# The passage from the scan to the second feed-forward layer: sums of squares carried on by VectorE, transposes pinned to products, three units by token halves

## The chip, the cores and the metric

One Trainium2 chip, one of its cores. The kernel is one program on one core; its time is the device time of one execution in microseconds (us). The time before is the median of three executions, 740.4 us (739.77 to 740.83). The profile comes from one more execution.

Engines in the rows: PE is TensorE (PEld its weight loads, which overlap), DVE is VectorE, ACT is ScalarE, POOL is GpSimd, SP is SyncE, which here issues the weight DMAs. A row's tile names are the program's; L61 is line 61 of the kernel.

## The reference

A decoder trunk on 256 tokens of width 1024, in float32, two layers. Each layer is a token mixer and then a gated feed-forward with a causal depthwise convolution of width 3. Layer 0 mixes by sparse attention, layer 1 by a state-space scan (SSD). Each of the four sub-layers is wrapped in two RMS norms:

```
m = mixer(rms_norm(h, gains[0]));   h = h + rms_norm(m, gains[1])
f = conv_ffn(rms_norm(h, gains[2])); h = h + rms_norm(f, gains[3])

rms_norm(x, g) = x * rsqrt(mean(x*x, axis=-1) + 1e-6) * g
conv_ffn(h) = (silu(gate) * val) @ w_down,  [val, gate] = causal_dwconv(h @ w_up)
```

The change lies between the scan's output product (`ssd_mixer`'s `y @ w_out`) and the up-products `h @ w_up` of layer 1's feed-forward, whose hidden width is 2816 (22 units of 128 value and 128 gate columns).

## The kernel before, in words

**Arithmetic.** Every float32 operand is split into two float32r parts: `hi` is a rounded copy, made by ScalarE, and `lo = x - hi`, made by VectorE or GpSimd (`split`, line 55). A product of two such operands is three matmuls, hi*hi, hi*lo and lo*hi (`mm3`, line 166). Weights arrive by SP's DMAs in 512 KB parts (128x1024 float32) in five `raw` buffers; each part is split into `whi` and `wlo`. A `raw` buffer is free for the next DMA when its `wlo` has been made. A unit's weights are two parts.

**Tokens.** The 256 tokens are two halves of 128 (half 0 and half 1). `h[0]`, `h[1]` hold the residual stream with tokens on the partitions. The feed-forward needs it with channels on the partitions, so the normed half is transposed by PE (8 transposes of 128x128 in two groups of four, line 152), and the transposed groups are split into `xhi`, `xlo`.

**The passage.** `ssd_out_phase` (line 784) makes the scan's output product in four groups, g = 0 to 3, for half 0 and then half 1; the last stretch does g = 2 and g = 3 together. VectorE adds each group's product, scaled, to `osb` (line 832). For each half, `after` (line 870) then does:

- `postnorm` (line 156): the sum of squares of `osb` in two ScalarE activations of 128x512 (line 126), two GpSimd operations on 128x1 that add the two sums and EPS and take the power -0.5 (lines 117, 119), `fg = osb * gain` in two VectorE operations (line 161), and `h += fg * rstd` in two (line 164);
- `prenorm_steps` (line 141): the same sum of squares on `h`, the same two GpSimd operations, `xn = h * rstd * gain` in two VectorE operations (line 146), and then the transposes and splits.

Half 0's `after` is called before half 1's output products are written down in the program; half 1's `after` behind them.

**The first up-products.** In the feed-forward (`ffn`, line 536) the first two units are done by token halves (`proj_halves`, line 183): both units' products on half 0 (2 x 8 x 3 matmuls of 256 columns, tile `pv`), then half 1's transposes, then both units' products on half 1. A result by halves has tokens on the partitions, so ScalarE copies it to `ut` (line 181) and PE transposes it back (four 128x128 transposes a unit, line 202). All other units are done by `pair` (line 205) on both halves at once, with nothing to transpose.

**What sets the order.** A planner decides at build time in which order each engine gets its instructions: of those whose inputs are ready in its own estimate, it issues the one that stands first in the program's text. Each engine then runs its list strictly in order. `tc.issue_after(ins)` adds only a lower bound: what is written in its block comes behind `ins` in the list of that engine. `pend` (line 861) hands half 1's transposes such bounds: the first two products of the last eight on half 0 (`FB`). Half 0's transposes have no bound in this passage; in the passage from the first feed-forward layer to the scan they are bounded by two of half 1's last five products (`FA`, lines 573 and 574). A layer's tiles lie in a pool that is opened when the pool of the layer before has been closed; both use the same memory.

## Time and profile before

| what | value |
|---|---|
| median of three executions | 740.4 us (739.77 to 740.83) |
| the profiled execution | 737.78 us |
| its span, first to last instruction | 736.0 us |
| granted TensorE clock, mean of the span | 0.993 |
| PE busy | 713.1 us, 97% of the span |
| DVE / ACT / POOL busy | 567.2 / 466.7 / 75.8 us |
| the second feed-forward layer's first product starts | at 541.57 us |
| its last product starts | at 729.32 us |

Read it by stretches: the shares of the whole span are averages over layers with different limits. The `windows` view gives, for each stretch, how long each engine was busy, with the number of instructions in parentheses. The `timeline` view gives single instructions in order of time; a bracket at the end of a row is the time that the engine sat idle before it and what ended that. A row with `x2` merges two that follow each other.

### The profile page before, as it was taken

The page shows a single profiled execution, that of the slowest core. Times are in us where ns is not written, and L with a number is a line of the kernel's source. Part 1 is how long each engine was busy: PE and PEld are TensorE (multiplying, and loading weights), DVE is VectorE, ACT ScalarE, POOL GpSimd, SP SyncE. Part 2 cuts the span into 40 slices and gives each one's busy share as a digit, 9 for nine tenths or more (in the row PEclk, how much of TensorE's full clock was granted, in tenths as well). Part 3 has the DMA queues.
Part 4 walks back from the last instruction along what each step waited for, and adds up shares of the span by engine and source line. Part 5 has one row for each costly group of instructions (what it writes and reads, how often), then busy time and mean ns, then how long its engine had stood idle before and what let it go on. Part 6 is the DMA issues. An engine that isn't in the chain of part 4 may idle for free.

```text
span 736.0 us, 13745 instructions
## 1 busy us (share of the span) xinstructions
PE 713.1 (97%) x5252; PEld 658.0 (89%) x5252; DVE 567.2 (77%) x994; ACT 466.7 (63%) x879; POOL 75.8 (10%) x113
## 2 busy tenths in 40 slices
PE   7998999999999999999999999999989999999996
PEld 4998986779999999997999999998779999999995
DVE  4688898667867777688698878898888877767783
ACT  5577997447656555566776687765647655555551
POOL 2321442120000000001000000133120000000000
PEclk8999999999999999999999999999999999999998
DMA  8865431425655665564445574144655656555531
GB/s 313 297 220 181 140 119 59 142 79 185 199 197 173 193 202 182 195 218 154 139 166 172 181 232 133 58 139 148 200 172 172 200 175 200 197 185 189 181 106 57
DMA packets 35426, 126.07 MB, mean 171 GB/s; under 512 B 4065, under 2 KB 4385, under 8 KB 35361
## 3 DMA queue, kind: packets, MB, share of 16 engines
q1 hardware_dynamic: 35360, 125.20, 51.9%
q8 instruction: 41, 0.67, 0.4%
q14 instruction: 25, 0.20, 0.1%
HBM read 124.14 MB, written 1.05 MB: 170 GB/s over the span
## 4 chain that ended last, share of the span: by engine, by line
PE 77%; DVE 8%; ACT 7%; DMA 4%; issue 2%; POOL 1%; SPq 0%; DVEq 0%; POOLq 0%; ACTq 0%
PE pu L61 45%; PE acc L61 18%; PE pv L61 5%; DVE wlo L57 4%; ACT P L391 2%; PE pt L65 2%; ACT whi L56 2%; PE po L61 2%; ACT junk L126 1%; DMA raw<-in_nsa_in 1%; PE py L61 1%; DMA raw<-in_ffn_down 1%; DMA raw<-in_cmp_w 1%; DVE gw L799 1%; DMA raw<-in_ssd_out 1%
## 5 line engine op out<-in xcount | busy, mean ns | idle before, releaser
L57 DVE TENSOR_TENSOR wlo<-raw,whi 128x1024 fp32r<-128x1024 f32 (+1 forms) x219 | 270.5, 1240 | 79.9 <-ACT whi L56 79.2
L56 ACT CAST whi<-raw 128x1024 fp32r<-128x1024 f32 x223 | 230.8, 1045 | 111.0 <-PE pu L61 56.6
L61 PE MATMUL pu<-xhi,whi 128*128 128x256 f32 x1056 | 296.0, 281 | 1.5 <-DVE graw L288 1.5
L61 PE MATMUL pu<-xhi,wlo 128*128 128x256 f32 x1056 | 295.0, 280 | 1.5 <-DVE wlo L57 1.5
L61 PE MATMUL pu<-xlo,whi 128*128 128x256 f32 x1056 | 294.6, 279 | 0.0
L61 PEld LDWEIGHTS pu<-xhi,whi 128*128 128x128 f32 x1056 | 198.5, 188 | 3.4 <-ACT kd L358 1.6
L61 PEld LDWEIGHTS pu<-xhi,wlo 128*128 128x128 f32 x1056 | 198.4, 188 | 2.2 <-DVE wlo L57 2.1
L61 PEld LDWEIGHTS pu<-xlo,whi 128*128 128x128 f32 x1056 | 198.5, 188 | 1.2
L534 DVE SCALAR_TENSOR_TENSOR cc<-pu,pr,cc 128x255 f32<-128x255 f32 (+2 forms) x248 | 111.3, 477 | 6.7 <-ACT cc L528 3.6
L61 PE MATMUL acc<-whi,hm 128*128 128x512 f32 x352 | 114.6, 390 | 0.1
L61 PEld LDWEIGHTS acc<-whi,hm 128*128 128x128 f32 x352 | 66.1, 188 | 13.8 <-ACT hm L56 0.6
L61 PE MATMUL acc<-wlo,hm 128*128 128x512 f32 x176 | 68.9, 392 | 0.0
L528 ACT ACTIVATE cc<-pu,pr 128x256 f32<-128x256 f32 x112 | 57.8, 559 | 8.9 <-PE pu L61 8.8
L117 POOL TENSOR_SCALAR ms<-ss 128x1 f32<-128x1 f32 x16 | 7.9, 491 | 416.3 <-ACT junk L126 416.3
L56 ACT CAST hm<-cc 128x256 fp32r<-128x256 f32 x44 | 17.8, 404 | 44.9 <-DVE cc L562 44.9
L61 PE MATMUL acc<-whi,gw 128*128 128x512 f32 x128 | 41.3, 397 | 0.0
L61 PEld LDWEIGHTS acc<-wlo,hm 128*128 128x128 f32 x176 | 33.0, 188 | 5.6
L61 PE MATMUL pv<-whi,xhi 128*128 128x256 f32 (+1 forms) x128 | 36.8, 300 | 0.9 <-ACT xhi L56 0.4
L61 PE MATMUL pv<-whi,xlo 128*128 128x256 f32 (+1 forms) x128 | 35.5, 294 | 1.0 <-DVE xlo L57 0.9
L61 PE MATMUL pv<-wlo,xhi 128*128 128x256 f32 (+1 forms) x128 | 35.2, 285 | 0.2 <-DVE wlo L57 0.2
L391 ACT ACTIVATE P<-P,mx 128x128 f32<-128x128 f32 (+1 forms) x64 | 28.3, 447 | 2.9 <-DVE mx L389 2.9
L57 DVE TENSOR_TENSOR hm<-cc,hm 128x256 fp32r<-128x256 f32 x44 | 18.6, 424 | 14.6 <-ACT hm L56 14.6
(205 smaller groups left out, 862.7 us busy)
## 6 DMA issues: line engine op xcount, KB each, us to landing
raw<-in_ffn_up SPq DMA_DIRECT2D x88, 512.0 KB, 4.3
raw<-in_ffn_down SPq DMA_DIRECT2D x44, 512.0 KB, 4.6
raw<-in_ssd_in SPq DMA_DIRECT2D x40, 512.0 KB, 4.4
raw<-in_nsa_in SPq DMA_DIRECT2D x18, 512.0 KB, 5.1
raw<-in_ssd_out SPq DMA_DIRECT2D x16, 512.0 KB, 4.3
gain<-in_gains SPq DMA_DIRECT2D x8, 512.0 KB, 4.7
raw<-in_cmp_w SPq DMA_DIRECT2D x8, 512.0 KB, 6.3
raw<-in_nsa_out SPq DMA_DIRECT2D x8, 512.0 KB, 3.7
```

The costliest lines, as they stand in the source:

```text
L56: r = copy(hi, src)
L57: eng.tensor_tensor(lo, src, hi.bitcast(F32), op=OP.subtract)
L61: last_mm[0] = nc.tensor.matmul(*a, **k)
L65: last_mm[0] = nc.tensor.transpose(*a)
L117: nc.gpsimd.tensor_scalar(ms, a, b, EPS, op0=OP.mult if isinstance(b, float) else OP.add, op1=OP.add)
L126: nc.scalar.activation(junk, src[c], AF.Square, scale=1.0 / 32, accum_out=ss[:, c:c + 1])
L391: nc.scalar.activation(p, p, AF.Exp, scale=-1.0, bias=mx[:, qt, b:b + 1], accum_out=sums[:, qt, hh, b + 1:b + 2])
L528: nc.scalar.activation(c, ps, AF.Identity, bias=pr[:, base + nt:base + nt + 1], scale=pr[:, base + nt - 1:base + nt])
L534: nc.vector.scalar_tensor_tensor(c[:, s:], ps[:, :S - s], wv, c[:, s:], op0=OP.mult, op1=OP.add)
L799: nc.vector.scalar_tensor_tensor(gw[1][:, t, :], gg[:, t, :], nw, gw[0][:, t, :].bitcast(F32), op0=OP.mult, op1=OP.subtract)
```

## The change

It touches this one passage.

- **`rms_chain`** replaces `rms` in `postnorm` and `prenorm_steps` there. ScalarE squares the first 512 columns only; VectorE adds EPS to that sum and goes on with the second 512 columns in a `tensor_tensor_reduce` that starts from it; GpSimd only takes the power. Of the two `fg = osb * gain` the first goes to GpSimd.
- **Half 0's transposes** are written down behind half 1's output products and bounded by the fourth and the fifth of the last eight (`marks[3:5]`); before, they stood ahead of those products, with no bound.
- **Three units** of the second feed-forward layer are done by token halves (`N1` = 3) where there were two. The third one's split weights go to the layer's own pool (`fp`, 4 buffers).
- **The weight splits** of these units are bounded, and three go to GpSimd: unit 0's two `wlo` stay on VectorE behind half 0's `xn`; unit 1's two and unit 2's first go to GpSimd behind half 0's second power; unit 2's second stays on VectorE, behind half 1's last `h`.

```diff
-T0, T1, N0, N1, SFILL, LAG = 5, 4, 2, 2, 2, 5
+T0, T1, N0, N1, SFILL, LAG = 5, 4, 2, 3, 2, 5
...
+    def rms_chain(src):
+        ss = tiny([128, 2], "ss")
+        junk = sp.tile([128, 512], BF16, name="junk", tag="junk", bufs=2)
+        nc.scalar.activation(junk, src[0], AF.Square, scale=1.0 / 32, accum_out=ss[:, 0:1])
+        junk = sp.tile([128, 512], BF16, name="junk", tag="junk", bufs=2)
+        nc.vector.tensor_scalar(ss[:, 0:1], ss[:, 0:1], EPS, None, op0=OP.add)
+        nc.vector.tensor_tensor_reduce(junk, src[1], src[1], 1.0 / 1024, ss[:, 0:1], OP.mult, OP.add, ss[:, 1:2])
+        r = tiny([128, 1], "rstd")
+        edge["pow"] = nc.gpsimd.tensor_tensor(r, ss[:, 1:2], mhalf, op=OP.pow).ins
+        return r
...
-    def postnorm(i, f, g):
+    def postnorm(i, f, g, rms=rms):
         t = sp.tile([128, D], F32, name="fg", tag="xn", bufs=2)
-        r = rms(f)
+        r = None if rms is rms_chain else rms(f)
         for c in range(2):
             cs = slice(512 * c, 512 * c + 512)
-            nc.vector.tensor_tensor(t[:, cs], f[c], g[:, cs], op=OP.mult)
+            if c and r is None:
+                r = rms(f)
+            eng = nc.gpsimd if rms is rms_chain and c == 0 else nc.vector
+            eng.tensor_tensor(t[:, cs], f[c], g[:, cs], op=OP.mult)
         for c in range(2):
             cs = slice(512 * c, 512 * c + 512)
-            nc.vector.scalar_tensor_tensor(h[i][:, cs], t[:, cs], r, h[i][:, cs], op0=OP.mult, op1=OP.add)
+            edge["h"] = nc.vector.scalar_tensor_tensor(h[i][:, cs], t[:, cs], r, h[i][:, cs], op0=OP.mult, op1=OP.add).ins
...
         ex = max(tail, 2 * nf - 4)
         hs, wd = {}, {}
-        first = proj_halves([weights(ffn_up[NP * l + p], KT, 256, *((fp, ex) if p >= 2 else ())) for p in range(nf)], xt, fp) if nf else None
+        if l:
+            a, b, c = edge["xn", 0], edge["pow", 0], edge["h"]
+            how = [((a, a), ()), ((b, b), (0, 1)), ((b, c), (0,))]
+        else:
+            how = [((), ()), ((), ())]
+        first = proj_halves([weights(ffn_up[NP * l + p], KT, 256, *((fp, ex) if p >= 2 else ()), order=o, lows=lows)
+                             for p, (o, lows) in enumerate(how)], xt, fp)
...
                     marks = out_mm(acc, i, jobs, True, True)
+                    if g == 3 and i and n:
+                        first_rows(marks[3:5])
...
                 if g == 3:
-                    after(i, [osb[:, i, :512], osb[:, i, 512:]], (None, None))
+                    first_rows = after(i, [osb[:, i, :512], osb[:, i, 512:]], (None, None), rms_chain)
...
-            postnorm(i, f, g[0])
+            postnorm(i, f, g[0], rms)
             if n < 8:
-                steps = prenorm_steps(i, g[1], xt_next, pins if i == 0 else pinned)
-                next(steps)
-                if i == 0:
+                places = list(pins) if i == 0 else pinned
+                steps = prenorm_steps(i, g[1], xt_next, places, rms)
+                edge["xn", i] = next(steps)[0]
+                if i == 0 and rms is rms_chain:
+                    edge["pow", 0] = edge["pow"]
+                    def rest(marks):
+                        places[:] = marks
+                        list(steps)
+                    return rest
+                elif i == 0:
                     list(steps)
                 else:
                     waiting.append(steps)
```

## Rows read from the trace of the kernel before

**Rows 1.** Windows view: stretch, its length, busy time of each engine, clock, DMA.
```profile
528.00:540.00 12.00, 10.52 (x51) 8.35 (x50) 10.37 (x15) 8.53 (x15) 3.04 (x4) 1.00 0.40 139
540.00:552.00 12.00, 10.43 (x78) 9.46 (x77) 9.44 (x13) 4.67 (x12) 2.02 (x4) 1.00 0.53 175
552.00:580.00 28.00, 27.99 (x238) 27.74 (x238) 24.08 (x40) 20.28 (x34) 0.00 (x0) 1.00 0.59 187
580.00:720.00 140.00, 140.00 (x990) 130.98 (x989) 102.98 (x154) 79.74 (x118) 0.00 (x0) 1.00 0.54 174
```
**Rows 2.** Waits of PE, 500 to 600 us: total us, times, longest.
```profile
PE pt L65 <- DVE xn L146: 3.0, 2, 1.6
```
**Rows 3.** Timeline of PE around half 0's transposes.
```profile
534.43 0.40 PE L61 MATMUL acc<-wlo,gw 128*128 128x512 f32 x1
...
536.31 0.63 PE L65 MATMUL pt<-ident,xn 128*128 128x128 f32 x4 [1.48 <-DVE xn L146]
...
537.36 0.47 PE L61 MATMUL acc<-whi,gw 128*128 128x512 f32 x1
...
541.57 0.28 PE L61 MATMUL pv<-whi,xhi 128*128 128x256 f32 x1
```
**Rows 4.** Timeline of PE around half 1's transposes.
```profile
547.24 0.38 PE L65 MATMUL pu<-ident,ut 128*128 128x128 f32 x2
...
549.18 0.66 PE L65 MATMUL pt<-ident,xn 128*128 128x128 f32 x4 [1.55 <-DVE xn L146]
```
**Rows 5.** Timeline of the other engines: half 1's chain from `osb` to `xn`.
```profile
541.52 1.40 DVE L832 SCALAR_TENSOR_TENSOR osb<-acc,rstd,osb 128x512 f32<-128x512 f32 x2
...
543.84 0.46 POOL L117 TENSOR_SCALAR ms<-ss 128x1 f32<-128x1 f32 x1 [8.46 <-ACT junk L126]
...
548.37 1.41 DVE L146 SCALAR_TENSOR_TENSOR xn<-h,rstd,gain 128x512 f32<-128x512 f32 x2 [0.85 <-POOL rstd L119]
```
**Rows 6.** Timeline of PE in the passage from the first feed-forward layer to the scan.
```profile
345.69 0.39 PE L61 MATMUL acc<-whi,hm 128*128 128x512 f32 x1
...
345.92 1.03 PE L65 MATMUL pt<-ident,xn 128*128 128x128 f32 x8
...
347.39 0.39 PE L61 MATMUL pv<-whi,xhi 128*128 128x256 f32 x1 [0.44 <-ACT xhi L56]
...
348.24 0.38 PE L61 MATMUL pv<-whi,xlo 128*128 128x256 f32 x1
```
**Rows 7.** Chain that ended last, 525 to 560 us: start, us, what.
```profile
556.71 0.22 PE pu L65 x2
```
**Rows 8.** Groups by line and form, whole span: busy us, mean ns; idle before.
```profile
L56 ACT CAST whi<-raw 128x1024 fp32r<-128x1024 f32 x219 | 227.8, 1050 | 111.0 <-PE pu L61 56.6 <-PE acc L61 34.9 <-DMA raw<-in_ffn_down 4.3
...
L57 POOL TENSOR_TENSOR wlo<-raw,whi 128x1024 fp32r<-128x1024 f32 x5 | 12.3, 2473 | 39.1 <-ACT whi L56 39.1
...
L802 POOL TENSOR_TENSOR sq<-sq 128x512 f32<-128x512 f32 x4 | 5.4, 1340 | 11.5 <-ACT sq L801 11.5
...
L389 DVE CUSTOM_DVE_ANT_0 P<-sa,cn 128x256 f32<-128x256 f32 x32 | 12.2, 416 | 0.8 <-PE sa L61 0.8
...
L389 DVE CUSTOM_DVE_ANT_0 P<-sb,cn 128x128 f32<-128x128 f32 x32 | 8.0, 281 | 1.7 <-PE sb L61 1.6
```
**Rows 9.** Timeline: a split on GpSimd beside one on VectorE, in the attention layer.
```profile
64.63 2.40 POOL L57 TENSOR_TENSOR wlo<-raw,whi 128x1024 fp32r<-128x1024 f32 x1 [12.33 <-ACT whi L56]
...
65.53 2.57 DVE L57 TENSOR_TENSOR wlo<-raw,whi 128x1024 fp32r<-128x1024 f32 x1
```
**Rows 10.** Timeline: half 0's passage: two splits, GpSimd's addition, `xn`.
```profile
532.28 2.35 DVE L57 TENSOR_TENSOR wlo<-raw,whi 128x1024 fp32r<-128x1024 f32 x2
...
533.33 1.39 POOL L117 TENSOR_SCALAR ms<-ss 128x1 f32<-128x1 f32 x1 [2.41 <-ACT junk L126]
...
535.41 1.42 DVE L146 SCALAR_TENSOR_TENSOR xn<-h,rstd,gain 128x512 f32<-128x512 f32 x2 [0.78 <-POOL rstd L119]
```
**Rows 11.** DMA issues, 500 to 580 us: count, KB each, median us to landing.
```profile
raw<-in_ffn_up SPq DMA_DIRECT2D x16, 512.0 KB, 4.7
```

More of the change, by code (lines that the diff above doesn't have):

```diff
@@ L66, in tr @@
         return last_mm[0]
-    last_mm = [None]
+    last_mm, edge = [None], {}
     class Weights:
@@ L139, in prenorm, with prenorm_steps @@
         return marks
-    def prenorm_steps(i, g, xt, pins):
+    def prenorm_steps(i, g, xt, pins, rms=rms):
         r = rms([h[i][:, :512], h[i][:, 512:]])
@@ L815, in scales @@
                 return rstd_of(sv, 1.0 / 512, 2)
-            todo.append((jobs, scales))
+            todo.append((jobs, scales, g))
             if g == 2:
@@ L821, in ssd_out_phase @@
             for i in range(2):
-                for n, (jobs, scales) in enumerate(todo):
+                for n, (jobs, scales, _) in enumerate(todo):
                     acc = [ps_([128, 512], "acc") for c in range(2)]
                     marks = out_mm(acc, i, jobs, True, True)
+                    if g == 3 and i and n:
+                        first_rows(marks[3:5])
                     if i == 0:
@@ L868, in boundary, with after @@
         g = {}
-        def after(i, f, pins=None):
+        def after(i, f, pins=None, rms=rms):
             if i == 0:
```

## The prediction

> **What bounds the kernel now.** I read the stretches first. In the second feed-forward layer PE does not rest: 27.99 us busy of 28 and 140.00 of 140, at the full clock [rows 1]. There the time is PE's work, and nothing can be hidden behind anything else. Ahead of it lie two stretches of 12 us in which PE is busy 10.52 and 10.43 us [rows 1]: 1.48 + 1.57 = 3.05 us idle. The view of waits says what for: two waits for `xn`, 3.0 us together [rows 2]. The timeline has them singly: 1.48 us ahead of half 0's transposes [rows 3] and 1.55 us ahead of half 1's [rows 4]. The clock is full in both stretches, so no loss from the clock can be won back. That makes 3.05 us the ceiling, unless PE is given less work, and it is given more.
>
> Why does PE wait? Half 0's transposes stand in PE's list 19 output products before the end (one product stands between their two groups of four, 18 behind), though `xn` is complete only at 535.41 + 1.42 = 536.83 [rows 3, 10]. Half 1's chain, from `osb` at 541.52 to `xn` at 548.37, takes 6.85 us [rows 5], and the two units' products on half 0 cover only 547.24 - 541.57 = 5.67 us of it [rows 3, 4].
>
> **The change part by part.** All sums are against the profiled execution, 737.78 us (span 736.0).
>
> *First wait, -1.48.* Half 0's transposes are now written behind half 1's products. The planner takes ready instructions in the order of the text, and a bound only says "not before"; products are ready, so I place the transposes behind all of them and not at the fourth. The other passage shows this: its transposes are bounded by two of the last five products, yet start at 345.92, directly behind the last product at 345.69 [rows 6]. The products then need no `xn`, and the wait goes. Between 537.36 and 541.57 there are 18 product starts, 0.234 us each [rows 3]. The 19 left, from 534.43 + 0.23 = 534.66 on, end at 539.1, which is 2.3 us behind today's `xn`.
>
> *What the new place costs, +0.8.* The first up-product now needs transposes that were just made. In the other passage this order gives 0.44 us idle, and then 0.85 us from the first `pv` to the first that needs `xlo`, filled with four products [rows 6]. Four take 4 x 5.67/48 = 0.47, so 0.38 is lost; together 0.82. The low end is 0 (transposes among the products, a rival below); the high end is another VectorE split of 1.22 ahead of `xlo`, about 2.0. I take 0.8, since that passage has the same order and the same tiles. The transposes themselves are in the sum before and after. Effective start of the up-products: 539.1 + (348.24 - 0.47 - 345.92) = 540.9.
>
> *Second wait, -1.55.* Three units instead of two put 72 products on half 0, 72 x 0.118 = 8.5 us, until 549.4. Half 1's chain starts with `osb`, at 539 to 540, and by its old length of 6.85 us has `xn` at 546 to 547, 2.5 to 3.5 us ahead of PE. The wait is covered with room to spare.
>
> *The chain itself, 0.* Per sum, a ScalarE square of 0.63 (a chain member in half 1) and a GpSimd addition of 0.46 [rows 5] go. VectorE gets one `tensor_tensor_reduce` of 128x512: the same instruction takes 281 ns at 128 columns and 416 at 256 [rows 8], so by 135 ns for each 128 about 0.69 us; and a 128x1 addition, surely under 0.28. One `fg` moves to GpSimd, where 128x512 takes 1.34 [rows 8], beside the square. So the chain gains some tenths or loses some: -0.4 to +0.3 for each sum. As it ends 2.5 us early, I cost it at nothing. If that cover went, all of it would count.
>
> *The third unit by halves, +0.5.* The number of products is the same, 48. New are four transposes of `ut`; two take 0.22 [rows 7] to 0.38 us [rows 4], so 0.44 to 0.76. I take 0.5. Their ScalarE copies lie beside products.
>
> *The splits.* On VectorE unit 0's two move behind `xn`: 536.83 + 2.35 = 539.2 [rows 10], needed at 540.9; room 1.7 us. On GpSimd three splits of 2.47 [rows 8] follow half 0's power: 535.4 + 7.4 = 542.8, and 544.1 with the 1.34 of `fg` between. Unit 1 is needed at 540.9 + 2.8 = 543.7, unit 2 at 546.6. So without collisions nothing is late. Collisions there will be: beside a GpSimd split a VectorE split took 2.57 instead of 1.2 us, +1.35 [rows 9], and beside two VectorE splits GpSimd's small addition took 1.39 instead of 0.46 [rows 5, 10]. In the window from 535 to 549 VectorE has up to nine operations with both inputs in SBUF that can meet the three splits. Cost on PE's path: 0 if the room of 1.7 and 2.5 us absorbs them, up to 2 x 1.35 = 2.7 if both of unit 0's splits are held, since `osb` and `xlo` stand behind them in VectorE's list. Nearest is a single hit, 1.35, which 1.7 absorbs all but wholly; I take +0.2.
>
> By the Trainium skill ("SBUF — State Buffer", section "Who interferes with whom") GpSimd shares one SBUF port pair with VectorE, as an exclusive lock: a VectorE instruction with two SBUF inputs and a GpSimd one that reads SBUF don't overlap at all. The trace agrees: GpSimd's split ended at 67.03, the VectorE split that started at 65.53 at 68.10, 1.07 later [rows 9]. By this rule moving a split to GpSimd takes nothing off the shared port, it asks for twice the time of it; this bears on the slower rival below.
>
> *SP's queue, 0.* `raw` buffers come free when their `wlo` is made, so unit 0's, now split about 4 us later, let the loads of unit 3 start as much later. A load lands in 4.7 us [rows 11], and these are needed when the pairs begin, behind 556.7 [rows 7].
>
> Sum: -1.48 + 0.8 - 1.55 + 0.5 + 0.2 = -1.53 us. The profiled execution lies 2.6 us below the median of the runs shown; I take the difference over unchanged: 740.4 - 1.5 = 738.9 us.
>
> **The rivals.**
>
> *A: the transposes do land among the products.* Then the 0.8 isn't paid, and neither is a split in the way of `xlo`: -1.48 - 1.55 + 0.5 = -2.5, 737.9 us. For it: before, the planner did put them among products [rows 3]. Against it: rows 6.
>
> *B: the third unit is late.* Its first split is the third on GpSimd, and its tile lies in a pool whose memory the layer before still uses until half 1's last reading of `osb`, about 541.5 to 543. Cast and split, 1.05 + 2.47 [rows 8], then end at 545 to 546.5 without a collision and 1.35 later with one, against 546.6 needed. PE waits up to 1.3 us: -1.53 + 1.2 = -0.3, 740.1 us. For it: GpSimd does everything in order, and the second power of half 1 stands in the same list. Against it: the pool may be freed early.
>
> *C: slower, the splits on GpSimd hold VectorE in front of the first up-products.* The place is 535.4, when half 0's power ends: `xn` on VectorE and unit 1's first split on GpSimd become ready together. If GpSimd goes first, `xn` waits 2.4 us, and unit 0's splits meet the next one, +1.35 to +2.7. It decides from the point where the hold exceeds 1.7 us. Two holds of 2.4 less 1.7 are 3.1 us on PE's path, and half 1's chain, three two-input steps behind three splits, loses its 2.5 us as well: -1.73 + 3.1 = +1.4, 741.8 us, up to 743. For it: the two collisions of rows 9 and 10. Against it: VectorE got both its splits through while GpSimd waited [rows 10]. By the lock in the Trainium skill's page ("SBUF — State Buffer", "Who interferes with whom") whichever starts first keeps the port for its whole length, so which of the two starts first at 535.4 would decide it.
>
> **How the numbers follow.** The forecast 0.55, A 0.12, B 0.15, C 0.18. A measurement of this kernel can tell about 0.2%, 1.5 us, from no change. The forecast's own range is 738.1 to 739.6 (0.8 to 2.3 us less), and about 0.33 of its 0.55 lies beyond 1.5 us. With A that is 0.45 faster. The same: 0.21 of the forecast, 0.13 of B, 0.04 of C, 0.38. Slower: 0.14 of C and some of B, 0.17. The range to hold eight in ten leaves out half of A at the bottom and the end of C: 737.7 to 742.0.
>
> **What would show it.** In the changed kernel's timeline: PE's output products run to about 539 without a break; the eight transposes stand directly behind them; no wait of `pt` for `xn` is left; 72 `pv` products in a row; GpSimd's splits between 535 and 545, and whether `xn`, `wlo` or `h` beside them take longer than now. PE's idle time in the passage should be 1.0 to 1.5 us instead of 3.05. The forecast is wrong if PE waits for `wlo` or `xlo` for more than 1 us, or if `xn` of half 0 ends behind 539.

## The result, and the profile after

The changed kernel is slower: 745.67 us, median of 9 runs (744.93 to 747.02), against 740.32 for the kernel before; ratio 1.0074, 95% interval 1.0063 to 1.0086. That is 5.4 us more, where I had forecast 1.5 less, and outside my range. The profiled execution took 744.93 us (span 743.1).

Where in the program? The same two instructions in both traces tell it (timeline of ScalarE: start, us, what): a square of the scan's output phase ahead of the passage, and a weight cast well inside the feed-forward layer. First the kernel before, then the changed one.
```profile
498.23 1.06 ACT L801 ACTIVATE sq<-xs 128x1024 f32<-128x1024 f32 x1 [2.15 <-PE pss L61]
...
603.38 1.05 ACT L56 CAST whi<-raw 128x1024 fp32r<-128x1024 f32 x1 [0.91 <-PE pu L61]
```
```profile
500.65 1.06 ACT L821 ACTIVATE sq<-xs 128x1024 f32<-128x1024 f32 x1 [2.14 <-PE pss L61]
...
610.49 1.05 ACT L56 CAST whi<-raw 128x1024 fp32r<-128x1024 f32 x1 [0.91 <-PE pu L61]
```
The first comes 2.42 us later, the second 7.11: the passage between them costs 4.69 us. The 2.42 lie ahead of the passage: up to there PE, VectorE, ScalarE and GpSimd execute the same instructions in the same order in both traces (last section). I give this "cost of the passage" for every kernel below; it is free of what differs elsewhere from run to run.

Stretches of the changed kernel (columns as in [rows 1]):
```profile
528.00:540.00 12.00, 12.00 (x54) 9.77 (x53) 10.85 (x16) 5.45 (x8) 6.66 (x8) 1.00 0.26 96
540.00:552.00 12.00, 6.87 (x34) 5.88 (x33) 11.14 (x15) 4.22 (x9) 4.15 (x4) 0.72 0.54 173
552.00:580.00 28.00, 27.74 (x233) 27.06 (x233) 23.55 (x37) 16.84 (x32) 3.63 (x2) 1.00 0.53 174
580.00:720.00 140.00, 140.00 (x1018) 132.10 (x1017) 106.09 (x158) 83.23 (x122) 0.00 (x0) 1.00 0.57 184
```
The first stretch has no idle time left (1.48 before), the second has 5.13 us of it and a clock of 0.72. VectorE is busy 11.14 us of 12. The waits of PE, which answer to [rows 2]:
```profile
PE pv L61 <- ACT xhi L56: 4.2, 1, 4.2
PE pt L65 <- DVE xn L157: 0.9, 1, 0.9
PE pv L61 <- DVE wlo L57: 0.2, 1, 0.2
```
The wait is named after `xhi`, the cast on ScalarE, but this only came last. The timelines show what was late first: GpSimd and VectorE, then ScalarE, then PE.
```profile
536.16 0.55 POOL L130 TENSOR_TENSOR rstd<-ss,mhalf 128x1 f32<-128x1 f32 x1 [2.67 <-DVE ss L128]
536.68 5.19 POOL L57 TENSOR_TENSOR wlo<-raw,whi 128x1024 fp32r<-128x1024 f32 x2
...
551.52 2.64 POOL L57 TENSOR_TENSOR wlo<-raw,whi 128x1024 fp32r<-128x1024 f32 x1 [1.08 <-ACT whi L56]
```
```profile
536.75 5.67 DVE L157 SCALAR_TENSOR_TENSOR xn<-h,rstd,gain 128x512 f32<-128x512 f32 x2
542.34 0.74 DVE L854 SCALAR_TENSOR_TENSOR osb<-acc,rstd,osb 128x512 f32<-128x512 f32 x1
543.00 2.34 DVE L57 TENSOR_TENSOR wlo<-raw,whi 128x1024 fp32r<-128x1024 f32 x2
545.27 1.40 DVE L854 SCALAR_TENSOR_TENSOR osb<-acc,rstd,osb 128x512 f32<-128x512 f32 x2
...
547.89 1.28 DVE L57 TENSOR_TENSOR xlo<-pt,xhi 128x512 fp32r<-128x512 f32 x2
...
551.81 3.43 DVE L57 TENSOR_TENSOR wlo<-raw,whi 128x1024 fp32r<-128x1024 f32 x1
...
557.68 1.42 DVE L157 SCALAR_TENSOR_TENSOR xn<-h,rstd,gain 128x512 f32<-128x512 f32 x2 [0.44 <-POOL rstd L130]
```
```profile
546.12 0.63 ACT L125 ACTIVATE junk<-osb 128x512 bf16<-128x512 f32 x1 [9.13 <-DVE osb L854]
...
546.75 1.05 ACT L56 CAST xhi<-pt 128x512 fp32r<-128x512 f32 x2
```
```profile
541.04 0.60 PE L65 MATMUL pt<-ident,xn 128*128 128x128 f32 x4
542.56 0.63 PE L65 MATMUL pt<-ident,xn 128*128 128x128 f32 x4 [0.92 <-DVE xn L157]
547.37 0.58 PE L61 MATMUL pv<-whi,xhi 128*128 128x256 f32 x1 [4.18 <-ACT xhi L56]
...
558.70 1.17 PE L65 MATMUL pt<-ident,xn 128*128 128x128 f32 x8
```
Half 0's power releases GpSimd's two splits of unit 1 and VectorE's two `xn` within 0.07 us of each other, GpSimd first. The two `xn` then take 5.67 us; before they took 1.42 [rows 10]. 4.25 us are lost in VectorE's list, with three `osb`, two splits and the rest behind them, and this list runs without a break until 546.7. ScalarE has the square of half 1's `osb` ahead of half 0's `xhi` and waits 9.13 us for it. So the first `pv` comes at 547.37, or 544.95 without the 2.42 us from ahead of the passage; I had expected 540.9. From 545.02, inside the wait of 4.18 us, the granted clock is half, 1.2 GHz:
```profile
545.02:551.85 6.83, 4.45 (x19) 0.50 0.92 294
```
(PE alone, clock, DMA.) The second wait [rows 4] is gone: half 1's transposes start at 558.70 with none. In sum: 5.3 us of waits instead of 3.0, some 2 us from 19 products at half clock, and the third unit's transposes, +4.8 against 4.69 measured.

### The profile page after: what moved, and what is told of

Its sections match the earlier page's. It is cut to its first block, busy times and chain, and to the rows that moved or that the text cites. A ratio compares the mean times of both kernels' runs of the same rounds, so it can differ in the third digit from the quotient of the medians.

```text
span 743.1 us, 13753 instructions
## 1 busy us (share of the span) xinstructions
PE 716.9 (96%) x5256; PEld 662.2 (89%) x5256; DVE 573.4 (77%) x1001; ACT 464.9 (63%) x873; POOL 83.8 (11%) x114
## 3 DMA queue, kind: packets, MB, share of 16 engines
HBM read 124.14 MB, written 1.05 MB: 168 GB/s over the span
## 4 chain that ended last, share of the span: by engine, by line
PE 80%; DVE 6%; ACT 6%; issue 3%; DMA 3%; POOL 1%; SPq 0%; DVEq 0%; POOLq 0%; ACTq 0%
PE pu L61 45%; PE acc L61 21%; PE pv L61 6%; DVE wlo L57 3%; PE pt L65 2%; ACT P L405 2%; ACT whi L56 2%; PE py L61 1%; PE po L61 1%; DMA gain<-in_gains 1%; DMA raw<-in_ssd_in 1%; DMA raw<-in_ffn_down 1%; DMA raw<-in_nsa_out 1%; ACT junk L137 1%; DVE xn L157 1%
## 5 line engine op out<-in xcount | busy, mean ns | idle before, releaser
L61 PE MATMUL pu<-xhi,whi 128*128 128x256 f32 x1040 | 291.6, 281 | 1.3 <-DVE graw L302 1.3
L61 PE MATMUL pu<-xhi,wlo 128*128 128x256 f32 x1040 | 290.6, 280 | 1.5 <-DVE wlo L57 1.5
L61 PE MATMUL pu<-xlo,whi 128*128 128x256 f32 x1040 | 290.2, 279 | 0.0
L61 PEld LDWEIGHTS pu<-xhi,whi 128*128 128x128 f32 x1040 | 195.5, 188 | 3.2 <-ACT kd L372 1.4
L61 PEld LDWEIGHTS pu<-xhi,wlo 128*128 128x128 f32 x1040 | 195.4, 188 | 2.2 <-DVE wlo L57 2.1
L61 PEld LDWEIGHTS pu<-xlo,whi 128*128 128x128 f32 x1040 | 195.5, 188 | 1.2
L61 PE MATMUL pv<-whi,xhi 128*128 128x256 f32 (+1 forms) x144 | 42.5, 306 | 5.2 <-ACT xhi L56 4.6
L61 PE MATMUL pv<-whi,xlo 128*128 128x256 f32 (+1 forms) x144 | 40.8, 300 | 1.0 <-DVE xlo L57 0.9
L61 PE MATMUL pv<-wlo,xhi 128*128 128x256 f32 (+1 forms) x144 | 41.4, 298 | 0.2 <-DVE wlo L57 0.2
L61 PEld LDWEIGHTS pv<-whi,xhi 128*128 128x128 f32 x144 | 28.4, 202 | 6.6 <-ACT xhi L56 5.6
```

Of the source, the lines that this page charges most:

```text
L61: last_mm[0] = nc.tensor.matmul(*a, **k)
```

## The experiments

Each ran beside the kernel before on the same chip. The difference is that of the medians; the ratio, with its 95% interval, is an estimate of its own over the same runs, so the two can part by some tenths, in e8 by a microsecond. "Half clock" is the length of that stretch in the passage, "waits" PE's waits from 520 to 600 us. The kernel before has waits of 3.0 and no half clock there. In all but e4, e7, e8, e11 and the changed kernel 0.2 to 0.6 us of the waits is one for `wlo` at 520 to 525 us, ahead of what the edits touch. Passage, waits and half clock are those of the one profiled execution, the difference is over all runs; as the clock varies among executions, the two can part by 2 us (e11). The expectations' times of the changed kernel count from 0.5 us later than the rows above. The edits are shown shortened.
```
                              diff us  ratio   95%             passage  waits  half clock
changed                        +5.4   1.0074  1.0063-1.0086    +4.69    5.3    6.8
e1  vector_splits              +1.9   1.0027  1.0012-1.0041    +1.89    2.7    3.4
e2  split_after_xn             +5.3   1.0067  1.0050-1.0084    +4.74    5.4    6.8
e3  square_later               +5.3   1.0075  1.0054-1.0096    +5.45    6.0    6.8
e4  old_chain                  +6.6   1.0088  1.0069-1.0106    +5.65    5.9    6.8
e5  three_units                +0.6   1.0005  0.9992-1.0018    +0.39    3.3    0
e6  chain_only                 +3.0   1.0034  1.0018-1.0051    +2.79    4.7    3.4
e7  transposes_only            -0.1   0.9998  0.9982-1.0013    -0.20    1.9    3.4
e8  products_in_wait           +5.5   1.0059  1.0040-1.0079    +4.71    3.8    0
e9  splits_left_out            +1.5   1.0018  1.0009-1.0027    +0.77    2.6    3.4
e10 old chain, vector splits    0.0   0.9990  0.9978-1.0002    +0.21    1.9    3.4
e11 lists_in_order             +2.2   1.0036  1.0020-1.0052    +3.96    4.0    6.8
e12 lists_and_product          +1.5   1.0012  1.0001-1.0023    +1.43    2.9    0
e13 left_out_and_product       +0.9   1.0006  0.9990-1.0021    +0.17    1.5    0
e14 cast_behind                +0.6   1.0008  0.9994-1.0021    +0.10    3.0    0
e15 cast_behind_and_product    -0.3   1.0000  0.9986-1.0015    +0.43    2.5    0
e16 hold_alone                 +5.9   1.0081  1.0066-1.0096    +5.55    6.3    6.8
e17 busy_without_reading       +0.8   1.0014  1.0001-1.0026    -0.08    3.4    0
```
My theory: GpSimd's splits take the shared SBUF port ahead of `xn` and everything else follows. Rivals: ScalarE's order, the chain, the third unit, the clock.

**e1, the splits back on VectorE.**
```diff
-            how = [((a, a), ()), ((b, b), (0, 1)), ((b, c), (0,))]
+            how = [((a, a), ()), ((a, a), ()), ((a, c), ())]
```


> The changed kernel with the three splits of units 1 and 2 moved from GpSimd back to VectorE, bounded behind half 0's `xn`; all else as it is. Theory (the port): in the changed kernel's trace GpSimd's first split (536.17 us, 2.39) starts 0.07 us ahead of `xn` and its second (538.53, 2.83) follows at once, and the two `xn` take 2.88 and 2.87 where they take 0.75 alone, 4.3 us together; everything in VectorE's list behind them is late by that, and the 4.2 us wait of the first `pv` comes of it. Without GpSimd's splits `xn` takes twice 0.75 again, the first place costs about 1.3 us of idle TensorE, no stretch at half clock follows there, and VectorE's own four splits (4 x 1.22) land in half 1's chain, which may then end some 2 us after the 72 products: 741.5 us (739.5 to 743). Rival 1 (the third unit by halves or the longer chain on VectorE is what costs): it stays at 744.5 or more, since both are still there. Rival 2 (the low clock alone, by itself): the half-clock stretch after 544 us is still there, and the time is 743.5 or more.


741.73: the theory's number, in part by luck. The new place costs 1.8 us of waits where 1.3 were expected, a half-clock stretch of 3.4 us remains that it had excluded, and half 1's chain, which it had up to 2 us late, is not waited for at all. On VectorE the three splits cost the kernel 3.5 us less than on GpSimd (+1.9 instead of +5.4). The two `xn` take 1.41 again:
```profile
537.74 1.41 DVE L157 SCALAR_TENSOR_TENSOR xn<-h,rstd,gain 128x512 f32<-128x512 f32 x2
```

**e2, GpSimd's splits behind `xn`.**
```diff
+            edge["seen"] = nc.gpsimd.tensor_copy(tiny([128, 1], "seen"), xn[:, D - 1:]).ins
-            a, b, c = edge["xn", 0], edge["pow", 0], edge["h"]
+            a, b, c = edge["xn", 0], edge["seen"], edge["h"]
```


> The changed kernel with one GpSimd instruction more: it copies the last column of half 0's `xn` (128x1), and the splits of units 1 and 2 stand behind it, so that GpSimd begins the same three splits only after both `xn`; VectorE's and ScalarE's lists are the same as in the changed kernel. Theory (which of the two engines begins first decides): `xn` takes 0.75 twice and ends near 537.7 us instead of 541.9; the hold of GpSimd's splits then falls on unit 0's two splits and one `osb`, with about 2 us of lateness at the first `pv` instead of the 4.2 us wait: 742 us (740.5 to 743.5). Rival (a split of GpSimd costs VectorE its 2.4 us wherever it lies): VectorE loses the same 4.3 us a little later, and the time is 744.5 or more.


745.12: here my theory was wrong and its rival right. `xn` is free (1.42), and so is the `osb` behind it, which has one of its two inputs in PSUM; unit 0's splits take the hold (timeline of GpSimd and VectorE):
```profile
537.56 5.67 POOL L57 TENSOR_TENSOR wlo<-raw,whi 128x1024 fp32r<-128x1024 f32 x2
537.28 0.75 DVE L856 SCALAR_TENSOR_TENSOR osb<-acc,rstd,osb 128x512 f32<-128x512 f32 x1
537.94 6.38 DVE L57 TENSOR_TENSOR wlo<-raw,whi 128x1024 fp32r<-128x1024 f32 x2
```
6.38 for two that take 2.34 alone, 4.0 us lost again. That `xn` went first saved nothing: VectorE's list has no free time here, and what it loses anywhere in it is lost to all that follows. Who begins first isn't tested by this: here too GpSimd's first split began ahead of VectorE's, by 0.38 us.

**e3, ScalarE's order.**
```diff
+                        edge["xhi"] = list(steps)[1][0]     # in rest(marks)
+        with after_ins(edge.pop("xhi", None)):               # half 1's osb
             nc.scalar.activation(junk, src[0], AF.Square, ...
```


> The changed kernel with the Square of half 1's `osb` bound behind half 0's two `xhi` casts in ScalarE's list (in the changed kernel's trace it stands ahead of them and runs at 545.61 us, while half 0's first transposes end near 541.6); GpSimd's splits stay. Rival to the port (ScalarE's list holds the casts back some 3 us): the casts run at 542 to 544 us, the first `pv` comes 2.5 us or more earlier, and the time falls to 742.5. Theory: the casts run earlier, but the `xlo` of half 0 still stands behind two splits, two `osb` and one `fg` in VectorE's list, which the held `xn` pushed to 547.4, and the third product needs it: 745.2 us, within 0.5 us of the changed kernel.


745.11: the rival falls. The longest wait is now named after `xlo` (3.7 us): the releaser in a view of waits can be changed without changing the wait.

**e4, the old chain.**
```diff
-                    first_rows = after(i, [osb[:, i, :512], osb[:, i, 512:]], (None, None), rms_chain)
+                    first_rows = after(i, [osb[:, i, :512], osb[:, i, 512:]], (None, None), rms_old)
```
(`rms_old` is `rms`, with its power named for the bound of the splits.)


> The changed kernel with the sums of squares as before, two Squares on ScalarE and the add of EPS and power on GpSimd, and both `fg` on VectorE; the three units, the place of the transposes and GpSimd's splits stay. Theory (the port): `xn` and GpSimd's first split are still released by the same power, within 0.2 us of each other, GpSimd takes the port, and the time stays within 1.5 us of the changed kernel's: 745 us (743.5 to 746.5). Rival (the chain on VectorE, with its 128x512 reduction of 0.74 us, its add of 0.15 and `fg` on GpSimd, makes half 0 late): the time falls by 2 us or more, to 742.5 or below.


746.45, near the theory: the two `xn` take 5.68 us beside GpSimd's 5.20. The chain is not what starts the loss.

**e5, three units alone** (kernel before, `N1` 3 instead of 2).


> The kernel before with one number changed: three units by halves instead of two (the third unit's splits on VectorE, no bounds); sums of squares and transposes as before. Theory (this part is sound by itself; the port and the low clock are what cost): the second wait of before, 1.55 us, goes or shrinks to half, the third unit's four transposes more cost 0.5, and the third unit's two splits (1.22 each) in half 1's chain give back up to 1: 739.8 us (738.8 to 741.3), within 1 us of before. Rival (the third unit by halves is itself what costs in the changed kernel): 743 or more.


741.17, as expected within its range, but no gain. PE's waits:
```profile
PE pt L65 <- DVE xn L146: 1.5, 1, 1.5
PE pv L61 <- ACT ut L181: 1.0, 1, 1.0
PE acc L61 <- DVE wlo L57: 0.4, 1, 0.4
PE pv L61 <- DVE wlo L57: 0.4, 1, 0.4
```
The second wait for `xn` is gone, and 1.0 and 0.4 us come in its place: the third product group needs the first one's bank, whose copy to `ut` stands behind a weight cast in ScalarE's list. The wait of `acc` is the one near 521 us.

**e6, the chain alone** (changed kernel; two units, no bounds, half 0's transposes at the old pins).
```diff
-                    if g == 3 and i and n:
-                        first_rows(marks[3:5])
-                if i == 0 and rms is rms_chain:
+                if i == 0 and rms is None:
-            how = [((a, a), ()), ((b, b), (0, 1)), ((b, c), (0,))]
+            how = [((), ()), ((), ())]
```


> The kernel before with the new chain alone: half of each sum of squares on VectorE, one `fg` column half on GpSimd, for both halves of the passage; two units by halves, their splits on VectorE, half 0's transposes pinned by the old places. Theory: the chain is no faster in VectorE's full list than the old one, since the reduction, the add and the wait for ScalarE (0.75, 0.15 and some 0.3) stand in VectorE's own list where it had two Squares on ScalarE; the waits of TensorE stay at 2.5 to 4 us, and the time within 1.5 us of before: 740.5 us (739 to 742). Rival (the chain is what makes the changed kernel slow): 743 or more. Rival (the chain is the good part): 738.5 or less.


743.48: the theory fails and its first rival holds; the chain does cost, 3 us by itself. PE waits 4.1 us for `xn` (3.4 at half 1):
```profile
PE pt L65 <- DVE xn L157: 4.1, 2, 3.4
```
The hold is in the chain as well. Beside the `fg` that went to GpSimd, VectorE's `fg` takes 1.06 us (0.67 alone) and a split 1.95 (1.22 alone); beside another split GpSimd's power takes 1.46 (0.55 alone). VectorE and GpSimd at half 1, with the first `fg` of half 0 ahead:
```profile
530.41 1.06 DVE L175 TENSOR_TENSOR fg<-osb,gain 128x512 f32<-128x512 f32 x1
...
543.53 1.95 DVE L57 TENSOR_TENSOR wlo<-raw,whi 128x1024 fp32r<-128x1024 f32 x1
...
546.74 1.21 DVE L57 TENSOR_TENSOR wlo<-raw,whi 128x1024 fp32r<-128x1024 f32 x1
```
```profile
543.10 1.30 POOL L175 TENSOR_TENSOR fg<-osb,gain 128x512 f32<-128x512 f32 x1 [5.72 <-DVE osb L851]
546.89 1.46 POOL L130 TENSOR_TENSOR rstd<-ss,mhalf 128x1 f32<-128x1 f32 x1 [2.49 <-DVE ss L128]
```

**e7, the transposes alone** (kernel before with `rest` and `first_rows`, old sums).
```diff
-                    after(i, [osb[:, i, :512], osb[:, i, 512:]], (None, None))
+                    first_rows = after(i, [osb[:, i, :512], osb[:, i, 512:]], (None, None), rms)
```


> The kernel before with half 0's transposes alone moved behind the output products of half 1; old sums of squares, two units by halves. Theory: the first wait of before, 1.48 us, goes, and the step transposes, `xhi`, `xlo` in front of the first up-product costs 1 to 2.5 us of idle TensorE, for nothing is left to issue there; the second wait stays: 741 us (739.5 to 743), with half clock behind the first place if its idle time comes together with the transposes' own. Rival (as I predicted: 1.48 gone for 0.8): 739.7 or less.


740.44, no change; the theory's range. The first wait is gone, the new place costs 1.36 for `xlo` and 0.24 for `xhi`, and then 3.4 us at half clock; of the second wait, which the theory left as it was, 0.32 remains:
```profile
542.07 0.39 PE L61 MATMUL pv<-whi,xhi 128*128 128x256 f32 x1 [0.24 <-ACT xhi L56]
...
544.18 0.38 PE L61 MATMUL pv<-whi,xlo 128*128 128x256 f32 x1 [1.36 <-DVE xlo L57]
```

**e8, products in the wait** (changed kernel).
```diff
                         first_rows(marks[3:5])
+                        d = pa([128, 512], "pk")
+                        with tc.issue_after(last_mm[0].ins):
+                            for k in range(4):
+                                mm(d, ident, cn[:, 0:512], start=k == 0, stop=k == 3)
```


> The changed kernel with four products more (128x512, fp32, of constant tiles into a spare bank, nobody reads the result), bound behind half 0's last transpose, in the place of the 4.2 us for which TensorE waits ahead of the first `pv`; VectorE's, ScalarE's and GpSimd's lists are those of the changed kernel. It tells what the half-clock stretch costs apart from the wait. Theory (the wait brings the granted clock from 1.00 to 0.50 at 544.5 to 551.3 us, and some 20 `pv` products at 0.213 us instead of 0.118 cost about 2 us): with the products in the wait the clock stays at 1.00, the first `pv` comes at the same time, and the time falls by 2 us, to 743.5 (742.5 to 744.5). Rival (what the clock takes is given back later, as VectorE's and GpSimd's work is late anyway): within 0.7 us of the changed kernel, 745 or more.


746.05: the rival. The clock stays full (the stretch, PE busy, clock, DMA), and nothing is won:
```profile
540.00:560.00 20.00, 16.19 (x97) 1.00 0.50 165
```
```profile
PE pv L61 <- DVE wlo L57: 1.4, 1, 1.4
```
The faster products arrive at unit 2's second split, 1.40 us before VectorE has made it. So in the profiled execution the half clock costs nothing net (the passage is +4.71 instead of +4.69), since VectorE is later still. One of the eight executions took 740.91 us, the others 744.96 to 747.00; why is open.

**e9, the splits of units 1 and 2 left out** (changed kernel).
```diff
+                if lows == "none":
+                    nc.scalar.copy(hi, raw)
+                    self.parts.append((hi, lent.parts[c // m][1]))
+                    continue
-            how = [((a, a), ()), ((b, b), (0, 1)), ((b, c), (0,))]
+            how = [((a, a), ()), ((), "none"), ((), "none")]
```


> The changed kernel with the low parts of units 1 and 2 left out: their products read unit 0's low parts instead (so the numbers are not the reference's), and neither GpSimd nor VectorE splits them; products, casts, loads, chain, three units and transposes stay. It tells what the change would be worth if the three splits cost nothing, as my sum had it. Theory (VectorE's list bounds the passage and the splits on GpSimd stretch it): `xn` of half 0 takes 0.75 twice, the first place costs about 1.3 us of idle TensorE as in the run with the splits on VectorE, half 1's chain ends before the 72 products do, and what is left over the kernel before is a half-clock stretch of 3.4 us (about 1.4 us): 740.5 us (739 to 741.8). Rival 1 (my sum as it stood, the splits apart): 739 or less. Rival 2 (the chain on VectorE costs its 2.8 us, as alone in the kernel before, even without those splits): 742 or more.


741.06, in the theory's range: with the splits free the change is still 1.5 us behind the kernel before (0.8 in the passage), not 1.5 ahead. So my sum lacked something else too.

**e10, old chain and splits on VectorE** (e4 with this edit, which also frees the splits of units 0 and 1 from their bounds).
```diff
-            how = [((a, a), ()), ((b, b), (0, 1)), ((b, c), (0,))]
+            how = [((), ()), ((), ()), ((c, c), ())]
```


> The changed kernel with the old chain and the splits of unit 1 and 2 on VectorE (unit 2's behind half 1's `h`): that is, only the three units and the moved transposes are left of the change. Theory: with neither GpSimd's splits nor the chain nothing of the loss is left; the two parts measured alone cost 0.4 and gain 0.2 us, so 740.3 us (739.2 to 741.5). Rival (the parts lose only together, by the half clock behind the moved transposes and half 1's late chain): 742 or more.


739.61, level with before. With e1 and e4 this makes a rough square: by the differences from the kernel before, GpSimd's splits cost 3.5 us with the new chain (+5.4 against +1.9) and 6.6 with the old (+6.6 against 0.0); the new chain costs 1.9 with the splits on VectorE, and with them on GpSimd its 1.2 less lie inside the intervals. It is rough because bounds differ too: two splits run ahead of `xn` in e10, as in the kernel before, and none directly ahead of it in e1 and e4.

**e11 and e12, VectorE's list by hand, and one product in the wait** (from e10).
```diff
+                        if g == 3 and i and n:
+                            with tc.issue_after(edge["lo"]):     # half 0's last xlo
+                                nc.vector.scalar_tensor_tensor(ob, acc[c], ...
-                    ps = pair(weights(ffn_up[NP * l + p], KT, 256), xt)
+                    ps = pair(weights(..., order=(edge["xl"], edge["xl"]) if l and p == nf else ()), xt)
```


> The kernel of the run before this one (old chain, three units, moved transposes, splits on VectorE) with VectorE's list set by hand: half 0's two `xlo` ahead of half 1's last two `osb`, and unit 3's splits only behind half 1's `xlo`. In the run with the transposes alone TensorE waits 1.36 us for `xlo`, which stands behind the two `osb`. Theory (VectorE's order, not its amount of work, costs there): the 1.4 us go, half 1's chain is 1.3 later and hidden by the 72 products, the split of unit 2's second half comes 1 to 2 us late behind half 1's `xn`: 739.5 us (738.3 to 741). Rival (each shift only moves the wait, since VectorE has no free time from 537 to 552 us): 740.3 or more.

> The same kernel with one fp32 product (128x512, constant tiles, nobody reads it) behind half 0's last transpose, which fills some 0.9 us of TensorE's wait for `xhi` and `xlo`. Theory: the half-clock stretch that follows the moved transposes goes or shortens, and about 1 us with it: 738.7 us (737.5 to 740). Rival (as with the four products in the changed kernel: what the clock gives back is waited for at VectorE's next result): within 0.5 us of the run without the product.


741.73 and 741.08: both forecasts fail, and e11's rival holds. Its premise was e7's wait for `xlo`; e10, where it starts from, waits 1.44 us for `xhi` and only 0.17 for `xlo`. The 0.17 goes, 1.48 for `xhi` stays, and half 1's `osb` and `h` come later: the third group of `pv` waits 1.86 and 1.63 us for `ut`. The product takes away the half clock, and the passage falls from +3.96 to +1.43; the medians differ by 0.65 only, so e12's mechanism is neither shown nor refuted.

**e13, e9 with two products** in the wait of 2.31 us (as in e8, two instead of four).


> The run with the low parts of units 1 and 2 left out (741.06 us), and two fp32 products of constant tiles (128x512, nobody reads them) behind half 0's last transpose, in its wait of 2.31 us for `xhi`; VectorE's and ScalarE's lists are the same. Theory (the 1.3 us that are left over the kernel before are the half-clock stretch of 3.4 us behind that wait, some 15 products at 0.21 us instead of 0.12): the clock stays at 1.00, half 1's `xn` is ready more than a microsecond ahead of its transposes there, so nothing takes the gain back: 739.7 us (738.8 to 740.6). Rival (the chain and the third unit's transposes are what is left): 740.8 or more.


741.14, in the rival's range, with an interval of 0.9990 to 1.0021: the total alone doesn't tell the two apart. In the passage it is +0.17 instead of +0.77, with the clock full: there the half clock accounts for 0.6 us of e9's rest.

**e14 and e15, a cast out of the way, and one product** (from e10).
```diff
+                    with after_ins(edge["xhi"] if l and p == nf else None):
+                        w = weights(ffn_up[NP * l + p], KT, 256)
-        pv = pa([128, 256], "pv")
+        pv = (ps_ if wide else pa)([128, 256], "pv")       # wide: unit 2, half 0
```


> The old chain, three units, moved transposes and all splits on VectorE (739.61 us), and two edits: unit 3's casts on ScalarE only behind half 0's `xhi` (there one of them, 1.04 us, stands in front of `xhi` and the first `pv` waits 1.44 us), and the third unit's first product group in another bank, so that it doesn't wait for the first unit's copy to `ut`. Theory: the wait for `xhi` falls by 0.8 us, but the third product then waits for `xlo` in VectorE's list, so 0.3 us are left of it: 739.3 us (738.3 to 740.3). Rival (the cast was what held the passage): 738.6 or less.

> The same with one fp32 product of constant tiles (128x512) behind half 0's last transpose. Theory: the half-clock stretch goes (1.4 us), the product adds at most 0.5 to the wait it fills, and half 1's `xn` comes before its transposes by the third unit's cover: 738.4 us (737.4 to 739.5), under both kernels. Rival (VectorE's next result takes it back, as in the changed kernel): 739.3 or more.


740.82 and 739.92: no gain, e14 above its range, e15 its rival's. In e14 the wait for `xhi` fell from 1.44 to 0.24, and 1.38 for `xlo` took its place (0.17 in e10); the clock was full in both, so e15's theory lacked its object. No kernel here beats the kernel before by more than the measurement can tell.

**e16 and e17, the hold alone** (kernel before).
```diff
+                if i == 0 and n == 6:
+                    with tc.issue_after(power[0]):
+                        for k in range(2):
+                            nc.gpsimd.tensor_tensor(xt[1][:, k], h[1]..., xt[0][:, k]..., op=OP.subtract)   # e16
+                            nc.gpsimd.memset(xt[1].bitcast(U32), 0)                                        # e17
```


> The kernel before with two GpSimd subtractions more (128x1024, fp32, both inputs in SBUF, into a dead tile), bound behind half 0's second power, where `xn` of half 0 becomes ready; nobody waits for their result, and the lists of the other engines stay as they are. Theory: the two have the length of two splits (2.4 us each), take the port 0.1 us ahead of `xn` and keep it alternately, so the two `xn` take about 2.9 us each instead of 0.75, half 0's transposes come 4.3 us later, and TensorE, which has nothing else there, waits 4.3 us longer: 744.8 us (743.8 to 746.5 with a half-clock stretch behind it). Rival (the hold is absorbed, and the lists the planner made for the changed kernel cost it): 741.5 or less.

> The same place, with two memsets of 128x2048 words into the dead tile instead of the subtractions (about 1.9 us each by the memset of 64x2112 words, 1.86 us, at the kernel's start): GpSimd is as busy, but reads nothing. One split stands one place earlier in VectorE's list. Theory (it is the reading of two inputs from SBUF on both engines that collides): `xn` takes 0.75 as before, and the time is that of the kernel before: 740.4 us (739.3 to 741.5). Rival (any long GpSimd work there delays VectorE, or half 1's addition behind it in GpSimd's list): 742.5 or more.


745.93 and 740.84. GpSimd and VectorE in e16, then in e17:
```profile
537.44 5.10 POOL L882 TENSOR_TENSOR xlo<-h,xhi 128x1024 fp32r<-128x1024 f32 x2
...
537.50 5.59 DVE L146 SCALAR_TENSOR_TENSOR xn<-h,rstd,gain 128x512 f32<-128x512 f32 x2 [0.77 <-POOL rstd L119]
```
```profile
538.72 3.67 POOL L882 MEMSET xlo<- 128x2048 uint32 x2
...
538.81 1.41 DVE L146 SCALAR_TENSOR_TENSOR xn<-h,rstd,gain 128x512 f32<-128x512 f32 x2 [0.78 <-POOL rstd L119]
```
With the order of VectorE's list unchanged, two subtractions that nobody waits for cost the kernel 5.9 us: `xn` loses 4.2, PE's waits are 3.3 us longer (0.4 of it ahead of the place, near 521 us), and a stretch of 6.8 us at half clock begins at 540.25. GpSimd work of 3.67 us that only writes leaves `xn` at 1.41 and the passage at -0.08. The total of e17 is 0.8 higher, with an interval that begins at 1.0001; its passage shows none of it.

## Why the prediction was wrong

*First wait, -1.48: right in kind.* The products run to 541.04 without a break and the transposes stand behind all of them; rival A is out. In e10 no wait of `pt` is left.

*What the new place costs, +0.8: too small.* Without GpSimd's splits it was 1.6 (e7, e10, e14), 1.8 (e1) and 2.3 us (e9): the other passage [rows 6], from which I took 0.8, has no `osb` and no weight splits ahead of `xlo` in VectorE's list. I had named 2.0 as its high end. The half clock behind it is not in my sum at all; I had taken the full clock of [rows 1] for granted.

*Second wait, -1.55: right in kind.* e5 and the changed kernel have no such wait of PE for half 1's `xn`, but e8 shows that in the changed kernel another, for unit 2's `wlo`, stood right in front of it. That is rival B's place: 0.24 us in the changed kernel, where everything ahead of it is late, and 1.40 in e8.

*The chain itself, 0: wrong, +3.0 alone* (e6; about 1.9 from e10 to e1, with other bounds). The sizes were right (the reduction 0.75, the addition 0.15, [rows 8] gave 0.69 and under 0.28). I priced them as if VectorE were free when their inputs are ready. They stand in its list among `osb`, `fg` and splits, and the `fg` given to GpSimd holds that list besides (e6: 1.06 instead of 0.67, 1.95 instead of 1.22).

*The third unit, +0.5: too small.* e5 should have come out at -1.05 with the second wait and came out at +0.39: PE's waits there hold 1.0 for a bank and 0.4 for a split that I had not seen.

*The splits, +0.2: this step failed most; 3.5 measured* (e1), more with the old chain. The step bounded collisions at 2 x 1.35, from [rows 9], with 1.7 us of room to absorb them. But 1.35 was a split that met the last 1.5 us of another; each `xn` that starts together with a GpSimd split loses 2.1. And the hold came ahead of the room: with `xn` at the head of the list, unit 0's splits ended at 545.34 (542.9 without the 2.42) instead of 539.2, with the last `osb`, ScalarE's square of it and `xlo` behind them. Rival C had the place and the mechanism (0.18), with the price too low, since it subtracted the 1.7. It also held that who starts first decides; in these meetings GpSimd always began first, so that stays untested.

*SP's queue, 0:* PE has no wait that is named after a load. But with unit 0's splits late no load of weights is issued from 527.00 to 544.27 (in the kernel before 524.93 to 533.52, in e1 527.98 to 541.01), and ScalarE waits 1.65 us for one, until 549.46; what that costs isn't shown.

Shown: the hold by itself costs the kernel before 5.9 us (e16), it is absent where GpSimd only writes (e17), and moving the splits back to VectorE gives back 3.5 of the changed kernel's 5.4 us (e1; 2.8 of 4.7 in the passage). By the Trainium skill ("SBUF — State Buffer", section "Who interferes with whom") a VectorE instruction with two SBUF inputs contends with a GpSimd one that reads SBUF, not with one that only writes it, and the later one blocks fully; e16 and e17 agree, but for 0.6 us: e16's four instructions end 5.65 us after the first began, where their lone times add to 6.2. What remains, 1.5 to 1.9 us (e9, e1; 0.8 to 1.9 in the passage), is the dearer place of the transposes, the chain and some half clock; how it splits among these stays open, since their effects are not additive (the chain costs 3.0 alone and nothing that can be told beside GpSimd's splits).

Why no part gains is argued, not shown: VectorE is busy 21.54 us of the 28 from 528 to 556 in the kernel before, 23.81 in e10 and 25.95 in the changed kernel (of which 4.25 are lost in the held `xn` and 2.2 in a held split). Shown is that a wait taken away at one place comes back at VectorE's or ScalarE's next result (e8, e11, e14).

## What to carry to other kernels

Work moved from VectorE to GpSimd is not taken off VectorE where GpSimd reads SBUF and VectorE's instructions beside it have two inputs there: count GpSimd's time as a delay of them (4.0 to 4.25 us for two splits of 2.4 here), and of all that stands behind them in VectorE's list. A chain step's price is its duration plus its place in an in-order list, so list, for a passage like this one, everything that each engine has in order before costing a step at nothing. A hold is told from mere business by a control on the same engine that writes but doesn't read.

## What was not expected of the hardware

Beside each other the two engines take turns, each almost in full: in the changed kernel two splits of 2.4 us and two `xn` of 0.7 (6.2 together) ended 5.74 us after the first began, and in e2 two splits on either engine, 2.4 and 1.2 us each alone (7.1 together), took 6.76. It works the other way as well: GpSimd's power of 128x1 took 1.47 us instead of 0.55 beside a VectorE split in the changed kernel (start 556.18).

The granted clock fell to half behind waits of 1.03 and 0.56 us (e1) and of 0.24 and 1.36 (e7) that follow the transposes, but not in e14, whose waits are alike (0.24 and 1.38); why is open. It also falls in places that no kernel here changed: in e13 from 336 to 344 us the mean clock is 0.79 with PE busy 6.22 us of 8, behind a wait of 1.78 us for `hm`; in the kernel before it is 1.00 and 7.87 (stretch, PE busy, clock, DMA; e13, then before):
```profile
336.00:344.00 8.00, 6.22 (x21) 0.79 0.58 199
```
```profile
336.00:344.00 8.00, 7.87 (x35) 1.00 0.45 163
```
Such stretches are one reason why executions of one kernel differ (how much of their spread they make isn't shown), and why the cost of the passage, taken between two instructions of one trace, leaves out what a total holds.
